# Two-layer hybrid decoder: triangular inverses started from 16x16 blocks made row by row, mixer products kept in DRAM until wanted, batch ends behind the next front, PSUM banks shared out anew

## The chip, the cores and the metric

One Trainium2 chip, one core of it. The metric is the device time of one execution in microseconds; before the change the median of 3 runs is 2915.05 us (2909.9 to 2915.27).

## The reference, cut to what matters

256 tokens of width 2048 in f32 pass two layers. Each layer has a token mixer and a SwiGLU part, each as `LayerNorm(ALPHA * x + (1 + gate(c)) * f(x * (1 + scale(c)) + shift(c)))`, where shift, scale and gate come from `silu(c) @ ada_w` (192 pieces of 1 MB). The mixer of layer 0 ("AB") is one input projection, then 8 mLSTM heads of width 128 beside 16 RWKV-7 heads of width 64, then one output projection. The mixer of layer 1 ("CD") has 8 retention heads beside 8 gated DeltaNet (GDN) heads. The two parts of it that the change is about:

```python
# RWKV-7, per head, over all 256 tokens
S_t = S_{t-1} (diag(w_t) - kk_t (a_t*kk_t)^T) + v_t k_t^T ;  y_t = S_t r_t
# gated DeltaNet, per head and chunk: a unit triangular solve
ut = eye + where(strict, (kb @ kc^T) * gamma, 0)
u, w = triangular_solve(ut, v * beta), triangular_solve(ut, kb * exp(gc))
```

Both need, for each head and each chunk of 128 tokens, the inverse of a unit triangular 128x128 matrix: 8 such matrices in each of 4 RWKV batches (4 heads by 2 chunks) and of 2 GDN groups.

## The kernel before, in words

**Products.** Every weight matrix goes through `split` (L325-341): a 1 MB piece `raw` is loaded by SP's queue, ACT copies it to `hi` (fp32r, L337) and DVE subtracts to `lo` (L338), and each product of 128 tokens by 512 columns is three matmuls, hi by hi, lo by hi, hi by lo (L357 to L359). `product` takes two banks of kind "g" in PSUM, one for each half of the tokens, and sums 4 pieces into them, 96 matmuls for 512 columns. Between the pieces `ada` does a share of the 192 adaLN pieces on DVE (L289). A splitting runs with a priority 2000 ahead of its place in the program, so DVE and ACT make `hi` and `lo` as far ahead as buffers allow. The order on each engine is set by the scheduler of the tile framework, from the program order and such offsets; the pools set when a buffer is free.

**Mixer AB** (L1263). `first_products` makes four products while the first weights arrive. `rwkv` then runs four batches. A batch is `rwkv_batch` (low-rank gates), two times `rwkv_front` (channel work on 128 channels), then `rwkv_heads`: score matrices (L776 to L779), the masks on POOL (`keep_upper` L642, `unit_diagonal` L646), `inverses` (L600), the chunk recurrence (L793 to L819), and, in the same function, the batch's end (head norm, gate, L821 to L845). Products 3, 4 and 5 of the RWKV columns stand in the program between the batches; then come the mLSTM gates (L906ff) and two groups of four mLSTM heads (`mlstm_group`, L973), each with its own four products (`product(0)` to `product(3)`) in front of and between its steps. `mix_out` is the output projection: its first half sums the RWKV channels (weights `o_ab`), its second half the mLSTM channels.

**An inverse** (L600-639). For 8 matrices `mt` (transposed, unit upper triangular), `d` holds the inverses of the diagonal blocks and `dt` their transposes, first of 2x2 blocks: 8 transposes of `mt` (L611), a mask on DVE (L612) and one on POOL (L613). Then six levels, each doubling the block: 8 matmuls of 64 columns (L622), a mask on DVE (L626), 8 more (L629), an addition on DVE (L632), 8 transposes (L636), two copies on ACT (L637). Each matmul of 64 columns is two records in the trace, a transpose is one.

**PSUM banks**: 4 of kind "g" (products), 3 of "m", 1 of "c".

## Time and profile before

| | before |
|---|---|
| median of 3 runs | 2915.05 us (2909.9 to 2915.27) |
| the profiled execution, its own time | 2917.53 us |
| its span, first to last instruction | 2914.8 us |
| mean granted TensorE clock | 0.976 of full speed |
| PE (TensorE) busy | 2760.8 us, 95% |
| DVE (VectorE) busy | 2011.9 us, 69% |
| ACT (ScalarE) busy | 1276.3 us, 44% |
| POOL (GpSimd) busy | 123.5 us, 4% |
| DMA | 674.62 MB, 231 GB/s over the span |

Busy shares are of the span. Matmuls overlap in the pipe, so a matmul's own duration (395 ns for 512 columns) is longer than the distance from one start to the next (227 ns), and it is the distances that add up to the time. The span begins with some 150 us in which weights arrive; mixer AB then lasts to about 800 us, a SwiGLU part to about 1530 us, mixer CD to about 2200 us, and a SwiGLU part to the end.

### The profile page before, as it was taken

How to read it: one execution, taken by the hardware profiler on the slowest of the kernel's cores; microseconds unless marked ns; L12 is line 12 of the kernel's file. 1: busy time of each engine (PE TensorE's matmuls, PEld its weight loads, DVE VectorE, ACT ScalarE, POOL GpSimd, SP SyncE). 2: the span in 40 equal slices, each digit the busy share in tenths (PEclk: the TensorE clock that was granted, in tenths of full speed). 3: DMA queues.
4: the chain of work that ended last, by engine and by line, in shares of the span. 5: the costliest groups of instructions: out<-in, count | busy, mean ns of one | idle time of the engine just before them, and what ended most of it. 6: DMA issues, size and time to landing. Idle time of an engine off the chain costs nothing.

```text
span 2914.8 us, 34843 instructions
## 1 busy us (share of the span) xinstructions
PE 2760.8 (95%) x13466; PEld 2291.6 (79%) x13466; DVE 2011.9 (69%) x2955; ACT 1276.3 (44%) x1685; POOL 123.5 (4%) x114
## 2 busy tenths in 40 slices
PE   3699999999999999999998999999989999999997
PEld 2578887877778888888887888877878888888886
DVE  7876666687777557767758878687786545556556
ACT  2264345446454444444445545343444444443442
POOL 0001111020000000000000121101000000000000
PEclk9799999999999999999999999999999999999998
DMA  9974234367578668867855756477656656667563
GB/s 366 356 277 170 91 134 159 131 242 267 199 249 305 249 219 296 297 236 275 305 197 205 295 209 241 159 277 295 216 202 231 249 195 224 242 220 241 192 216 130
DMA packets 106189, 674.62 MB, mean 231 GB/s; under 512 B 12068, under 2 KB 14248, under 8 KB 28328
## 3 DMA queue, kind: packets, MB, share of 16 engines
q1 hardware_dynamic: 106024, 672.41, 64.1%
q8 instruction: 105, 1.72, 0.2%
q14 instruction: 60, 0.49, 0.0%
HBM read 663.97 MB, written 8.39 MB: 231 GB/s over the span
## 4 chain that ended last, share of the span: by engine, by line
PE 62%; DVE 5%; DMA 3%; issue 1%; ACT 1%; POOL 1%; POOLq 0%; DVEq 0%; ACTq 0%
PE g L359 19%; PE g L358 19%; PE g L357 19%; DMA raw<-ada 2%; DVE lo L338 2%; DVE raw L289 1%; PE m L622 1%; PE m L629 1%; PE m L575 1%; ACT hi L337 1%; DMA raw<-gu 1%; DMA raw<-w_cd 0%; PE m L524 0%; PE c L317 0%; PE m L636 0%
## 5 line engine op out<-in xcount | busy, mean ns | idle before, releaser
L338 DVE TENSOR_TENSOR lo<-raw,hi 128x1024 fp32r<-128x1024 f32 (+2 forms) x848 | 1025.4, 1215 | 653.6 <-ACT hi L337 650.3
L337 ACT ACTIVATE hi<-raw 128x1024 fp32r<-128x1024 f32 (+2 forms) x848 | 885.7, 1049 | 1165.6 <-PE g L359 1004.1
L357 PE MATMUL g<-hi,h 128*128 128x512 f32 (+3 forms) x2368 | 932.7, 396 | 80.3 <-ACT hi L337 76.5
L358 PE MATMUL g<-lo,h 128*128 128x512 f32 (+3 forms) x2368 | 934.1, 395 | 3.8 <-DVE lo L338 3.8
L359 PE MATMUL g<-hi,h 128*128 128x512 f32 (+3 forms) x2368 | 930.9, 394 | 0.0
L357 PEld LDWEIGHTS g<-hi,h 128*128 128x128 f32 x2368 | 451.9, 191 | 172.0 <-ACT hi L337 78.8
L358 PEld LDWEIGHTS g<-lo,h 128*128 128x128 f32 x2368 | 452.6, 191 | 95.2 <-DVE lo L338 9.1
L359 PEld LDWEIGHTS g<-hi,h 128*128 128x128 f32 x2368 | 452.0, 191 | 88.6 <-issue 2.7
L289 DVE SCALAR_TENSOR_TENSOR raw<-raw,silu_c 128x2048 f32<-128x2048 f32 x176 | 404.4, 2298 | 23.1 <-DMA raw<-ada 22.8
L359 PE MATMUL g<-hi,a 128*128 128x512 f32 x960 | 374.5, 390 | 0.0
L357 PE MATMUL g<-hi,a 128*128 128x512 f32 x960 | 374.4, 390 | 0.0
L358 PE MATMUL g<-lo,a 128*128 128x512 f32 x960 | 374.1, 390 | 0.1
L358 PEld LDWEIGHTS g<-lo,a 128*128 128x128 f32 x960 | 180.3, 188 | 37.4 <-DVE lo L338 0.5
L359 PEld LDWEIGHTS g<-hi,a 128*128 128x128 f32 x960 | 180.3, 188 | 36.9
L357 PEld LDWEIGHTS g<-hi,a 128*128 128x128 f32 x960 | 180.2, 188 | 37.0
L1099 POOL TENSOR_SCALAR s<-cons_sb,log_alpha 128x128 f32<-128x128 f32 x16 | 22.9, 1446 | 1040.6 <-PE g L359 903.4
L637 ACT ACTIVATE y<-m 128x512 f32<-128x512 f32 x48 | 27.4, 595 | 78.3 <-PE m L636 78.1
L902 DVE SCALAR_TENSOR_TENSOR f<-c,cols_sb,f 128x255 f32<-128x255 f32 (+2 forms) x120 | 57.2, 477 | 6.2 <-ACT f L900 5.1
L626 DVE TENSOR_TENSOR P<-m,cons_sb 128x256 f32<-128x256 f32 x72 | 30.1, 423 | 43.6 <-PE m L622 43.2
L629 PEld LDWEIGHTS m<-P,y 128*128 128x128 f32 x384 | 50.0, 203 | 2.1 <-issue 0.3
L622 PEld LDWEIGHTS m<-y,a 128*128 128x128 f32 x384 | 49.7, 205 | 0.8
L622 PE MATMUL m<-y,a 128*128 128x64 f32 x384 | 49.7, 283 | 0.0
(376 smaller groups left out, 2051.2 us busy)
## 6 DMA issues: line engine op xcount, KB each, us to landing
raw<-ada SPq DMA_DIRECT2D x176, 1024.0 KB, 5.5
raw<-gu SPq DMA_DIRECT2D x176, 1024.0 KB, 4.8
raw<-dn SPq DMA_DIRECT2D x88, 1024.0 KB, 4.8
raw<-w_cd SPq DMA_DIRECT2D x60, 1024.0 KB, 5.0
raw<-w_ab SPq DMA_DIRECT2D x56, 1024.0 KB, 5.5
a<-ada SPq DMA_DIRECT2D x16, 1024.0 KB, 11.3
raw<-o_ab SPq DMA_DIRECT2D x16, 1024.0 KB, 5.0
raw<-o_cd SPq DMA_DIRECT2D x16, 1024.0 KB, 4.9
```

What stands on the lines that cost most here:

```text
L289: v.scalar_tensor_tensor(w[:], w[:], 1.0, self.sc[:], ALU.mult, ALU.mult, accum_out=m[:, i:i + 1])
L337: nc.scalar.activation(hi[:, :2 * n], ws, AF.Copy)
L338: nc.vector.tensor_tensor(lo[:, :2 * n], ws, hi[:, :2 * n], ALU.subtract)
L357: mm(o, ah, wh, start=first, stop=False)
L358: mm(o, ah, wl, start=False, stop=False)
L359: mm(o, al, wh, start=False, stop=stop and k == 3)
L575: nc.tensor.transpose(b[:, P * k:P * k + P], gs[:, t, P * k:P * k + P], self.ident)
L622: nc.tensor.matmul(x[:, 64 * j:64 * j + 64], mt[:, hs.start + j, :], dv[:, hs.start + j, :, 0, :], start=True, stop=True)
L626: v.tensor_tensor(p[-1][:], four(x[:, 0:256]), mask, ALU.mult)
L629: nc.tensor.matmul(x[:, 256 + 64 * j:320 + 64 * j], dt[:, hs.start + j, :], y[:, j, :], start=True, stop=True)
L637: nc.scalar.activation(dt[:, hs, :], four(x[:]), AF.Copy)
L902: v.scalar_tensor_tensor(o[:, d:T], z[:, 0:T - d], self.col(wname, c + 3 - d), o[:, d:T], ALU.mult, ALU.add)
```

## The change: what it does

1. `inverses`: levels 2, 4 and 8 go (`LEVELS` is now 16, 32, 64). The inverses of the 16x16 diagonal blocks are made on DVE. Four masks take the diagonal 16x16 blocks of `mt` into `e2`, two operations form `u` (strictly upper) and `e` (with the diagonal), and 14 steps follow, one for each row k of the block from 14 down to 1: STREAM_SHUFFLE copies row k of each block to the 16 rows of it, a multiplication by column k of `u`, an addition into `e`, each over 128 partitions by 8 matrices by n = 1 to 14 columns. Then `dt` is spread from `e` by two multiplications, transposed (8 transposes), and copied to `d` by ACT. The chain has a priority 4000 ahead. `unit_diagonal` and POOL's masking of `mt` go, as does POOL's L613; `keep_upper` stays for the other score matrices.
2. Mixer AB: the mLSTM gates come first. Products 3 and 4 of RWKV follow batch 0, product 5 follows batch 1, and the eight mLSTM products follow batches 1 (one), 2 (three) and 3 (four), behind the heads of each. Nine of these products are put by: `put_by` copies each bank on ACT into `sp` (one buffer), and ACT's queue writes it to DRAM; `fetch` loads it on SP's queue when wanted. A batch's end (`rwkv_out`) stands behind the next batch's front.
3. Banks: 3 "g", 3 "m", 2 "c". `q4` has 4 buffers instead of 5 and `t1` 3 instead of 4; `sz`, the mLSTM tokens and the low ranks move to other pools, and retention's output takes its values' buffer. The first products take kinds gg, gm, mm, cc.

With three banks a product's first tile often takes the bank that was read last: in the order of the change, in the SwiGLU part, tile g_1378's last matmul is PE row 3347 and the first of g_1401, which takes its bank, is row 3360; with four banks, before, g_1391's last is row 3343 and its successor's first row 3446. Such a turn of 12 to 13 rows is that of about every second tile of the 224.

The diff, cut to its core:

```diff
-LEVELS = (2, 4, 8, 16, 32, 64)
+BASE = 16
+LEVELS = (16, 32, 64)
...
-        self.ps_g = pool("psg", 4, space=PSUM)
+        self.ps_g = pool("psg", 3, space=PSUM)
...
-        self.ps_c = pool("psc", 1, space=PSUM)
+        self.ps_c = pool("psc", 2, space=PSUM)
...
@@ inverses
+        with self.tc.high_priority(offset=4000):
+            e2 = self.t1([P, 8, 2, BASE])
+            for q in range(4):
...
+                v.tensor_tensor(e2[r], mt[r, :, r].rearrange("p h (a c) -> p h a c", a=2),
...
+            u, e, f = (self.own([P, 8, BASE], "e1", 3) for _ in range(3))
+            v.tensor_tensor(u[:], e2[:, :, 0, :], e2[:, :, 1, :], ALU.add)
+            v.tensor_tensor(e[:], u[:], self.con("diag").unsqueeze(1).to_broadcast([P, 8, BASE]), ALU.add)
+            for k in range(BASE - 2, 0, -1):
+                n = BASE - 1 - k
+                x = f[:, :, k + 1:]
+                v.stream_shuffle(x, e[:, :, k + 1:], [k] * 16 + [16 + k] * 16)
+                v.tensor_tensor(x, x, u[:, :, k:k + 1].to_broadcast([P, 8, n]), ALU.mult)
+                v.tensor_tensor(e[:, :, k + 1:], e[:, :, k + 1:], x, ALU.add)
         for hs in halves:
+            v.tensor_tensor(dt[:, hs, :].rearrange("p h (n c) -> p h n c", c=BASE), e[:, hs, :].unsqueeze(2).to_broadcast([P, 4, 8, BASE]),
+                            self.con("blk").unsqueeze(1).unsqueeze(3).to_broadcast([P, 4, 8, BASE]), ALU.mult)
             b = self.bank()
             for j in range(4):
-                nc.tensor.transpose(b[:, P * j:P * j + P], mt[:, hs.start + j, :], self.ident)
-            v.tensor_tensor(d[:, hs, :], four(b[:]), m2, ALU.mult)
-            nc.gpsimd.tensor_tensor(dt[:, hs, :], mt[:, hs, :], m2t, ALU.mult)
+                nc.tensor.transpose(b[:, P * j:P * j + P], dt[:, hs.start + j, :], self.ident)
+            nc.scalar.activation(d[:, hs, :], four(b[:]), AF.Copy)
...
+    def put_by(self, banks):
+        dst = self.dram.tile([T, 512], F32, name=self.name("by"))
+        for t in range(NT):
+            s = self.own([P, 512], "sp", 1)
+            self.nc.scalar.activation(s[:], banks[t][:], AF.Copy)
+            self.nc.scalar.dma_start(dst[P * t:P * t + P, :], s[:])
+        return dst
...
@@ rwkv_heads
-            self.keep_upper(mk[:, :, js, :], [2, 4], True)
-            self.unit_diagonal(mk[:, 0, js, :], 4)
+            self.keep_upper(mk[:, 1, js, :], [4], True)
...
+        return lambda: self.rwkv_out(B, yb)
...
@@ rwkv
+        for i in range(5):
...
+            if out:
+                out()
+            if i < 4:
+                out = self.rwkv_heads(B)
+            if i == 0:
+                tokens += [self.by_tokens(product(3 + j)) for j in range(2)]
+            elif i == 1:
+                tokens.append(self.put_by(product(5)))
+            after(i)
...
@@ mixer_ab
+        def after(i):
+            for _ in range((0, 1, 3, 4, 0)[i]):
+                cols.append(self.put_by(product(6 + len(cols))))
+            if i >= 3:
+                self.mlstm_group(i - 3, cols[4 * i - 12:4 * i - 8])
```

How it moves instructions, at three places. First PE at the start of the first inverse, from the second set of 4 transposes on (`m` a bank, `y` holding `d` and `dt`, `a` the matrices `mt`, `P` the masked product). Before, with levels 2 and 4:

```order
L611 MATMUL m_1061<-cons_sb,a_993 128x128 x4
L622 MATMUL m_1068<-y_1053,a_993 128x64 x4
L691 MATMUL c_1435<-cons_sb,a_825 128x128
L357 MATMUL g_2832<-hi_2840,h_140 128x512
...
L622 MATMUL m_1073<-y_1053,a_993 128x64 x4
L629 MATMUL m_1068<-P_1078,y_1053 128x64 x4
L357 MATMUL g_2833<-hi_2840,h_140 128x512
L629 MATMUL m_1073<-P_1080,y_1053 128x64 x4
L636 MATMUL m_1092<-cons_sb,y_1053 128x128 x4
...
L636 MATMUL m_1098<-cons_sb,y_1053 128x128 x4
L622 MATMUL m_1104<-y_1053,a_993 128x64 x4
```

In the change the first level is that of 16 (L642 and L649 are its matmuls, L656 its transposes):

```order
L632 MATMUL m_1147<-cons_sb,y_1093 128x128 x4
L632 MATMUL m_1154<-cons_sb,y_1093 128x128 x4
L362 MATMUL g_2278<-hi_2281,h_140 128x512
L642 MATMUL m_1160<-y_1093,a_1039 128x64 x4
L642 MATMUL m_1165<-y_1093,a_1039 128x64 x4
L360 MATMUL g_2277<-hi_2285,h_140 128x512
L787 MATMUL c_1702<-f_1695,cons_sb 128x256
L649 MATMUL m_1160<-P_1170,y_1093 128x64 x4
L649 MATMUL m_1165<-P_1172,y_1093 128x64 x4
...
L656 MATMUL m_1184<-cons_sb,y_1093 128x128 x4
L656 MATMUL m_1190<-cons_sb,y_1093 128x128 x4
L642 MATMUL m_1196<-y_1093,a_1039 128x64 x4
```

The transposes (now L632) take `dt` (in `y_1093`) instead of the matrices, so they stand behind the chain on DVE; three of the six sets of L622, L629 and L636 are gone.

Second, DVE at the same place in the change: the chain ahead of those transposes (`e_205` is `u`, `e_206` is `e`, `e_207` the shuffled rows; `a_1039` holds the matrices, `s_1094` is `e2`).

```order
L616 TENSOR_TENSOR s_1094<-a_1039,cons_sb 32x256 x4
L341 TENSOR_TENSOR lo_1604<-raw_1597,hi_1603 128x1024
L619 TENSOR_TENSOR e_205_1099<-s_1094 128x128
L813 COPY a_1040<-m_1079 128x256
L620 TENSOR_TENSOR e_206_1100<-e_205_1099,cons_sb 128x128
L341 TENSOR_TENSOR lo_2121<-raw_2118,hi_2120 128x1024
L624 STREAM_SHUFFLE e_207_1101<-e_206_1100 128x8
L813 COPY a_1040<-m_1085 128x256
L625 TENSOR_TENSOR e_207_1101<-e_207_1101,e_205_1099 128x8
L311 SCALAR_TENSOR_TENSOR one_and_gate<-modulation,cols_sb 128x4
L626 TENSOR_TENSOR e_206_1100<-e_206_1100,e_207_1101 128x8
L292 SCALAR_TENSOR_TENSOR raw_2152,modulation<-raw_2152,silu_c 128x2048
```

Between its links stand other instructions that DVE has ready, `lo` (L341) of 128x1024 and `ada` (L292) of 128x2048. From the last score copy before it to `dt`, 10 to 14 of the first and 5 or 6 of the second stand in an RWKV batch, and on PE 160 to 180 product matmuls of 512 columns.

Third, PE at the mLSTM heads. Before, between a head's weights (L955 to L959) and its output (L1000 to L1002):

```order
L957 MATMUL m_4270<-minus_m,cons_sb 128x256
L958 MATMUL m_4270<-cons_sb,s_4267 128x128
L959 MATMUL m_4270<-minus_m,cons_sb 128x128
L969 MATMUL m_4280<-y_3574 128x256
L970 MATMUL m_4280<-y_3574 128x128
L357 MATMUL g_4436<-hi_4522,h_496 128x512
L358 MATMUL g_4436<-lo_4523,h_496 128x512
L359 MATMUL g_4436<-hi_4522,h_496 128x512
...
L357 MATMUL g_4435<-hi_4555,h_674 128x512
L1000 MATMUL m_4284<-q_4111,t_4276 128x129
L1001 MATMUL m_4284<-q_4111,t_4276 128x129
L1002 MATMUL m_4284<-q_4111,t_4276 128x129
```

In the change (L1000 to L1004 are the weights, L1014 and L1015 the scores, L1041 to L1043 the output):

```order
L1002 MATMUL m_4660<-minus_m,cons_sb 128x256
L1003 MATMUL m_4660<-cons_sb,s_4657 128x128
L1004 MATMUL m_4660<-minus_m,cons_sb 128x128
L1014 MATMUL m_4670<-y_4547 128x256
L1015 MATMUL m_4670<-y_4547 128x128
L1041 MATMUL m_4674<-q_4624,t_4666 128x129
L1042 MATMUL m_4674<-q_4624,t_4666 128x129
L1043 MATMUL m_4674<-q_4624,t_4666 128x129
L1000 MATMUL m_4688<-cons_sb,s_4685 128x256
L1001 MATMUL m_4688<-cons_sb,log_f 128x128
L1002 MATMUL m_4688<-minus_m,cons_sb 128x256
```

No product stands between the four heads of the first group (rows 1847 to 1881), and in the second group the four heads have 0, 17, 1 and 15 product matmuls between scores and output; before, the eight heads had 5 to 118. In the stretch from the end of the fourth inverse to the second half of the output projection the change has some 200 product matmuls, most of them `o_ab`'s first half; before, the eight mLSTM products, 768 matmuls, ran beside the mLSTM steps as well.

## Rows read from the trace of the kernel before

**Rows 1.** The page, parts 1 and 2: busy time of each engine with its share of the span and its instructions.

```profile
PE 2760.8 (95%) x13466; PEld 2291.6 (79%) x13466; DVE 2011.9 (69%) x2955; ACT 1276.3 (44%) x1685; POOL 123.5 (4%) x114
```

**Rows 2.** Windows of the core: the stretch in us, busy us of PE, weight load, DVE, ACT and POOL (in brackets the instructions), granted TensorE clock, DMA share, GB/s. The first stretch is the load at the start, the others are the RWKV batches.

```profile
50.00:100.00 50.00, 29.30 (x125) 24.09 (x123) 42.74 (x47) 9.56 (x12) 0.00 (x0) 0.79 0.94 367
150.00:350.00 200.00, 191.79 (x1080) 159.32 (x1078) 137.24 (x253) 100.29 (x176) 22.12 (x18) 0.96 0.54 192
300.00:350.00 50.00, 46.48 (x257) 38.45 (x255) 29.71 (x64) 21.94 (x50) 10.30 (x9) 0.86 0.37 127
350.00:550.00 200.00, 194.00 (x1257) 166.28 (x1258) 125.94 (x292) 92.42 (x177) 21.59 (x19) 0.97 0.35 123
500.00:550.00 50.00, 47.29 (x328) 43.50 (x327) 27.89 (x55) 20.32 (x33) 6.97 (x8) 0.90 0.26 91
```

**Rows 3.** Timeline of PE in the SwiGLU part of layer 0: start us, duration us, engine, line, operation.

```profile
1000.01 0.39 PE L359 MATMUL g<-hi,a 128*128 128x512 f32 x1
1000.24 0.39 PE L357 MATMUL g<-hi,a 128*128 128x512 f32 x1
```

**Rows 4.** Timeline of PE in the first inverse, the same columns; x is how many records in a row.

```profile
250.68 1.90 PE L622 MATMUL m<-y,a 128*128 128x64 f32 x16
252.41 1.08 PE L724 MATMUL c<-cons_sb,b 128*128 128x256 f32 x4
...
256.05 1.04 PE L636 MATMUL m<-cons_sb,y 128*128 128x128 f32 x8
256.93 1.00 PE L622 MATMUL m<-y,a 128*128 128x64 f32 x8
```

**Rows 5.** The groups of PE by line, whole span: busy us, mean ns of one, idle us before and its releaser. The three levels' lines, for the RWKV batches (`y`) and the GDN groups (`a`).

```profile
L622 PE MATMUL m<-y,a 128*128 128x64 f32 x384 | 49.7, 283 | 0.0
L629 PE MATMUL m<-P,y 128*128 128x64 f32 x384 | 49.6, 284 | 0.0
L636 PE MATMUL m<-cons_sb,y 128*128 128x128 f32 x192 | 28.0, 280 | 0.0
...
L622 PE MATMUL m<-a,a 128*128 128x64 f32 x192 | 23.3, 272 | 0.0
L629 PE MATMUL m<-P,a 128*128 128x64 f32 x192 | 22.9, 271 | 0.0
...
L636 PE MATMUL m<-cons_sb,a 128*128 128x128 f32 x96 | 13.3, 273 | 0.0
```

**Rows 6.** The waits of the whole span: engine, tile and line, what it waited for, us in total, times, longest us.

```profile
ACT hi L337 <- PE g L359: 1004.1, 657, 8.4
...
PE m L524 <- DVE v L492: 18.5, 3, 6.2
...
PE m L611 <- POOL a L646: 16.9, 8, 3.9
```

**Rows 7.** The groups of DVE by line and shape, the same columns as in the groups of PE.

```profile
L338 DVE TENSOR_TENSOR lo<-raw,hi 128x1024 fp32r<-128x1024 f32 x824 | 1008.8, 1229 | 649.7 <-ACT hi L337 646.5 <-PE c L895 0.5
L289 DVE SCALAR_TENSOR_TENSOR raw<-raw,silu_c 128x2048 f32<-128x2048 f32 x176 | 404.4, 2298 | 23.1 <-DMA raw<-ada 22.8
...
L626 DVE TENSOR_TENSOR P<-m,cons_sb 128x256 f32<-128x256 f32 x72 | 30.1, 423 | 43.6 <-PE m L622 43.2
...
L632 DVE TENSOR_TENSOR y<-m,y 128x256 f32<-128x256 f32 x48 | 20.3, 424 | 25.2 <-PE m L629 24.8
...
L612 DVE TENSOR_TENSOR y<-m,cons_sb 128x512 f32<-128x512 f32 x8 | 5.5, 690 | 8.9 <-PE m L611 8.9
...
L412 DVE TENSOR_TENSOR v<-v 128x8 f32<-128x8 f32 x30 | 4.9, 164 | 0.5
...
L1191 DVE SCALAR_TENSOR_TENSOR s<-s,s 128x128 f32<-128x128 f32 x3 | 0.9, 291 | 0.1
```

**Rows 8.** The groups of ACT by line and shape, the same columns.

```profile
L637 ACT ACTIVATE y<-m 128x512 f32<-128x512 f32 x48 | 27.4, 595 | 78.3 <-PE m L636 78.1
```

**Rows 9.** Timeline of PE and DVE at the first two mLSTM heads: L970 is the end of a head's scores, L997 its weights times scores, L1000 its output; in square brackets idle us before and the releaser.

```profile
593.02 0.38 PE L970 MATMUL m<-y 128*128 128x128 f32 x2
...
598.17 0.80 PE L1000 MATMUL m<-q,t 128*128 128x129 f32 x2 [3.15 <-DVE t L997]
...
603.20 0.38 PE L970 MATMUL m<-y 128*128 128x128 f32 x2
...
604.61 0.56 DVE L997 SCALAR_TENSOR_TENSOR t<-m,t 128x384 f32<-128x384 f32 x1 [1.44 <-POOL t L642]
```

**Rows 10.** Timeline of PE, ACT and DVE at the end of products in the SwiGLU part: a product's last matmul into a bank, the copy that frees the bank, and the same on DVE (L572).

```profile
965.04 0.39 PE L359 MATMUL g<-hi,h 128*128 128x512 f32 x1
...
965.46 0.60 ACT L568 ACTIVATE q<-g 128x512 f32<-128x512 f32 x1 [0.30 <-PE g L359]
...
986.96 1.23 DVE L338 TENSOR_TENSOR lo<-raw,hi 128x1024 fp32r<-128x1024 f32 x1 [1.49 <-ACT hi L337]
988.10 1.28 DVE L572 TENSOR_TENSOR q<-g,q 128x512 f32<-128x512 f32 x2
```

**Rows 11.** The view of the DMA: issues by line and tile, KB each, median us from issue to landing (writes of 256 KB to DRAM).

```profile
x<-y SPq DMA_DIRECT2D x24, 256.0 KB, 2.8
```

More of the change, by code (lines that the diff above doesn't have):

```diff
@@ L46 @@
 _n = 0
-for _name, _w in [("ident", 128), ("cum", 256), ("tr", 128), ("ones", 128), ("sl", 128), ("m2", 128), ("m2t", 128),
+for _name, _w in [("ident", 128), ("cum", 256), ("tr", 128), ("ones", 128), ("sl", 128), ("tri", 32), ("diag", 16), ("blk", 8),
                   ("lev", 64 * len(LEVELS)), ("bones", 128), ("hsel", 2), ("freq", 64)]:
@@ L69, in constants @@
     put("sl", u > t)
-    put("m2", (u // 2 == t // 2) & (t <= u))
-    put("m2t", (u // 2 == t // 2) & (u <= t))
+    c32, c16 = np.arange(32)[None], np.arange(BASE)[None]
+    put("tri", (u % 32 // BASE == c32 // BASE) & (u % BASE < c32 % BASE))
+    put("diag", u % BASE == c16)
+    put("blk", u // BASE == np.arange(P // BASE)[None])
     lev = []
@@ L682, in by_tokens, with fetch @@
         return zt
+    def put_by(self, banks):
[5 more added lines that the diff above has]
+        return dst
+    def fetch(self, out, src):
+        for t in range(NT):
+            rows = src[P * t:P * t + P, :]
+            self.nc.sync.dma_start(out[:, t], rows if len(out.shape) == 3 else rows.rearrange("p (h d) -> p h d", h=4))
     def rwkv_tiles(self, zt, block):
         nc = self.nc
+        if block == 5:
+            src, zt = zt, self.own([P, NT, 512], "zt", 2)
+            self.fetch(zt, src)
         for i in range(0, 4, 2):
@@ L833, in rwkv_heads @@
                                  bias=va[:, j:j + 1], scale=rs[:, j:j + 1])
-        b = self.bank()
+        b = self.bank("c")
         for c in range(2):
@@ L853, in first_products @@
         srcs = [[low[i] for i in range(KG)]] + [[w[4 * b + i] for i in range(KG)] for b in range(3)]
-        banks = [[self.bank(k) for k in kinds] for kinds in ("gg", "gg", "mm", "mc")]
+        banks = [[self.bank(k) for k in kinds] for kinds in ("gg", "gm", "mm", "cc")]
         h = []
@@ L862, in first_products, with rwkv, conv @@
         return h, [banks[0], self.by_tokens(banks[1])] + [self.by_tokens(banks[2 + i], two[:, i]) for i in range(2)]
-    def rwkv(self, h, rate, early):
+    def rwkv(self, product, early, after):
         self.rkv = {}
         self.rwkv_low(early[0])
-        w = self.ins["w_ab"]
+        self.mlstm_gates()
+        nc = self.nc
         tokens = early[1:]
-        B = None
-        c = made = 0
-        for i in range(4):
-            while len(tokens) < (3, 3, 5, 6)[i]:
-                blk = len(tokens)
-                tokens.append(self.by_tokens(self.product([w[4 * blk + k] for k in range(KG)], 512, h, rate)))
-            B = self.rwkv_batch(i)
-            for c in (2 * i, 2 * i + 1):
-                while 4 * made < 3 * c + 3:
-                    self.rwkv_tiles(tokens[made], made)
-                    made += 1
-                self.rwkv_front(B, c)
-            if i % 2 == 0:
-                self.yT[2 + i // 2] = self.a8([P, 2, 4, T], F32R)
-            self.rwkv_heads(B)
-    def conv(self, banks, outs, wname, tile0):
+        made = 0
+        out = None
+        for i in range(5):
+            if i < 4:
+                B = self.rwkv_batch(i)
+                for c in (2 * i, 2 * i + 1):
+                    while 4 * made < 3 * c + 3:
+                        self.rwkv_tiles(tokens[made], made)
+                        made += 1
+                    self.rwkv_front(B, c)
+                if i % 2 == 0:
+                    y = self.yT[2 + i // 2] = self.a8([P, 2, 4, T], F32R)
+                    nc.gpsimd.memset(y[:, 0, 0, 0:1].bitcast(F32), 0.0)
+            if out:
+                out()
+            if i < 4:
+                out = self.rwkv_heads(B)
[4 more added lines that the diff above has]
+            after(i)
+    def conv(self, zt, outs, wname, tile0):
         nc, v = self.nc, self.nc.vector
-        zt = self.by_tokens(banks)
         for i in range(0, 4, 2):
@@ L1264, in mixer_ab, with product @@
         self.yT = {}
-        self.rwkv(h, rate, early)
-        self.mlstm_gates()
-        for g in range(2):
-            self.mlstm_group(g, self.ins["w_ab"], h, rate)
+        w = self.ins["w_ab"]
+        cols = []
+        def product(b):
+            return self.product([w[4 * b + k] for k in range(KG)], 512, h, rate)
+        def after(i):
[3 more added lines that the diff above has]
+                self.mlstm_group(i - 3, cols[4 * i - 12:4 * i - 8])
+        self.rwkv(product, early, after)
     def mixer_cd(self, h, rate):
```

53 lines of the change are left out of this document (25 added, 28 removed).

## The prediction

> **What bounds the kernel now.** I read the page first: PE is busy 95% of the span, DVE 69%, ACT 44%, POOL 4% [rows 1]. So the time goes where PE's time goes, unless an edit makes PE wait. Then the windows: while the weights first arrive PE is busy 29 of 50 us, and in the 400 us of the RWKV batches 191.79 and 194.00 of 200, so only 14 us of idle are to be had there [rows 2]. The timeline of a dense stretch gives the price of a product matmul of 512 columns: 0.23 us from one start to the next, not its duration of 0.39 [rows 3]. The same reading inside an inverse gives the price of a level [rows 4]. The waits show that PE's one systematic wait around the inverses is for POOL, 16.9 us in all, and that ACT, which makes `hi`, spends 1004 us waiting for PE [rows 6]: the splitting runs ahead of PE, and small delays on ACT or DVE reach PE only where that lead is used up.
>
> The profiled execution took 2917.5 us by its own time (span 2914.8), 2.5 above the median of 2915.05. The sum is made against 2917.5, and the 2.5 is taken off at the end. About 0.2% (6 us) is what a measurement of this kernel can tell from no change.
>
> **The change, part by part.**
>
> *Levels 2, 4 and 8 on PE.* One level is 16 records of L622, 16 of L629 and 8 of L636. Sixteen of L622 take 252.41 - 250.68 = 1.73 us; L629 has the same mean (284 against 283 ns), so 1.73 as well; eight of L636 take 256.93 - 256.05 = 0.88 [rows 4, 5]. Together 4.34 us. Three levels in six inverses are 18: **-78 us**. PE is full beside them with product matmuls that only move up, so the gain is real where PE stays full. By the records' durations the six levels are 186.8 us [rows 5], half of it 93; that counts the overlap of the pipe twice and is the far end. The near end is -60: in the inverse some of the removed time was a filler for a wait that stays.
>
> *POOL.* The transposes of the matrices no longer wait for POOL's masks: 16.9 us of wait in that form goes [rows 6]. What is late next is the DVE chain (below). I take **-12**; ends -17 and 0.
>
> *TensorE's clock.* The windows with an inverse's start show a granted clock of 0.86 and 0.90 [rows 2]. At 1.2 GHz instead of 2.4 for 28% and 20% of 50 us, PE loses at most 7 and 5 us. Fewer waits there give some of it back: **-5**; ends -12 and +5.
>
> *The DVE chain.* Each inverse gains 14 steps of three operations on 128 partitions by 8 to 112 elements. The trace has no shuffle; the nearest rows for all three are 164 ns at 8 columns and 291 ns at 128 [rows 7]. The mean step is at 60 columns, between them: 42 by 0.22 is about 9 us; ends 42 by 0.164 = 6.9 and 42 by 0.291 = 12.2. The masks and `dt` add 4 by 0.42, two small ones and 2 by 0.69, some 4 us; three levels of 2 by (0.423 + 0.424) and two operations of 0.69 go, 6.5 us [rows 7]. DVE has then about 6 us more per inverse, 38 in all on an engine that idles 31%. On the path it is the length of the chain that counts. In an RWKV batch the order puts 10 to 14 `lo` (1.23 us) and 5 or 6 `ada` (2.30 us) between its links [rows 7]: 9 + 4 + 12 by 1.23 + 5.5 by 2.30 is about 41 us, against 160 to 180 product matmuls of 0.227 us on PE, 36 to 41 us [rows 3]. So it is nearly covered. I take 1 us for each RWKV batch, none for the GDN groups: **+4**; ends 0 and +20. If the products ran out, all 41 us would be seen.
>
> The Trainium skill (VectorE: DVE Perf Modes, Rules for kernel authors) speaks against such a chain: every DVE operation drains the pipe, so in chained operations the count is to be kept down. The row of 164 ns for 8 columns agrees, since 16 times the columns cost only 1.8 times as much. By that rule alone 252 small operations for 18 levels would be a bad trade; by the sum it is one, only where DVE's time is not covered.
>
> *The mLSTM steps without their products.* Before, products stood between a head's scores and its output. In the change six of the eight heads have none or one there. Where seven product matmuls did not suffice, PE sat 3.15 us until 598.17, and from the scores' end at 593.40 it was 4.8 us; in the next head the output's operand was ready at 605.17, 1.6 us after the scores' end at 603.58 [rows 9]. So a bare head costs 1.6 to 4.8 us; six by 3.2 is 19. Each group also ends with a norm on DVE in front of its transposes; the nearest wait of PE for such a norm is at most 6.2 us [rows 6], and before, products filled it in part. I take 1 us for both: **+20**; ends 0 and 6 by 4.8 + 2 by 6.2 = +41.
>
> *Products put by.* Nine products by two copies of 0.6 us on ACT [rows 8]; some replace copies that were there. The second copy has one buffer `sp` and so waits for the first's write, 2.8 us [rows 11]. Behind it on ACT wait the next `hi`, and the bank stays taken meanwhile. Nine by 2.8 is 25 us of ACT; with 1004 us of ACT waiting for PE it mostly hides: **+5**; ends 0 and +25. The fetches, nine times 512 KB on SP's queue, stand behind weight loads and in front of others: no cost by themselves where DMA has room, 0.35 to 0.54 busy in the batches [rows 2].
>
> *Three banks for products.* Every second tile, 112 of 224, takes a bank whose last matmul is only 12 product matmuls back, 12 by 0.227 = 2.7 us [rows 3]. ACT freed one at 966.06, 1.0 us after its last matmul's start at 965.04; on DVE two in a row take 1.28 us, and may stand behind a `lo` of 1.23 [rows 10], 2.5 us. It just fits. **+4** for those behind an `ada`; the far end is a rival.
>
> *Batch ends behind the next front.* The 14 us of idle in the batches [rows 2] are nearly all POOL's, so **-2**.
>
> Sum: -78 - 12 - 5 + 4 + 20 + 5 + 4 - 2 = -64. 2917.5 - 64 - 2.5 is **2851 us**.
>
> **The rivals.**
>
> *The mLSTM stretch starves, and the clock with it* (2880). For it: DVE gets as much work there as PE, since the splitting and `ada` of the next weights run in it. The far end of the heads is +41 instead of +20. And PE with gaps has been granted 0.79 at the start, where it is busy 29 of 50 us [rows 2]; PE work of some 86 us (200 product matmuls are 45 of it) at 0.79 takes 23 us longer. Half of the latter with the former gives +31. Against: the heads are independent and may overlap. Chance 0.20. The Trainium skill (TensorE: Matmul & The Clock Gate, HAM oscillation) describes matmul loops that idle between bursts and start each burst cold; the window at the start agrees, and by it this rival's clock term would come in full.
>
> *DVE becomes the bound of the RWKV batches* (2888). At 0.34 a step (above the far row) and an `ada` in front of each link the chain is 46 us against 36 on PE: +9 or 10 in each of four batches. Chance 0.05.
>
> *More than the sum* (2815). The levels give 93, the waits of POOL and the clock all of theirs (17 and 12), the heads overlap. 2915 minus 122 plus some 20 for the rest is about 2815. For it: levels are chains between PE, DVE and ACT, whose cost beyond PE's own time also goes. Chance 0.16.
>
> *Slower: three banks* (2930). If the banks come free later than 2.7 us, behind a `lo` and an `ada` (1.23 + 2.30 + 0.68 = 4.2 us [rows 7, 10]), every such turn stalls PE. At 0.75 us for each of 112 turns that is +84, and eats the gain with 15 to spare. The point from which it decides is 64/112 = 0.57 us a turn. Against: ACT frees most banks in 1 us, and DVE idles. Chance 0.06.
>
> *Nothing to see* (2915). The removed levels only lay beside waits of the chain, and PE waits as long for DVE as it computed before. Chance 0.04; against it stands that PE is full in those stretches.
>
> **How the numbers follow.** The forecast itself has 0.49 (2830 to 2870). The range 2810 to 2888 takes in it, the starved stretch, DVE as the bound and most of the larger gain, and leaves out the two last rivals and some of the tails. All cases but those two are faster by over 0.2%: 0.90 faster, 0.04 the same, 0.06 slower.
>
> **What would show it.** Right: L642, L649 and L656 of the changed kernel with half the records of L622, L629 and L636; no wait of PE for POOL in the inverses; PE busy about 80 us less, the SwiGLU parts unchanged within some us. The heads show in the waits as PE L1041 waiting for DVE. Wrong: a wait of a product's first matmul for ACT or DVE evictions of tens of us (banks); transposes L632 waiting more than 5 us for DVE each (chain); a granted clock well under 1 in the mLSTM stretch; a mixer CD that loses as much as AB gains.

## The result, and the profile after

The changed kernel takes 2879.53 us (median of 4 runs, 2876.98 to 2886.5), before 2915.16 in the same comparison: a ratio of 0.988 with an interval of 0.986 to 0.991, or 36 us less. The forecast was 2851 with a range of 2810 to 2888, so the direction and the range held, but little more than half of the 64 us came: the time is that of the first rival, 2880. The profiled execution of the change took 2886.5 us, 7 above its median; its span is 2884.8. One of the four runs of the kernel with two products put by, below, took 4556.8 us at a granted clock of 0.555, and its ratio leaves that run out.

First the page's busy times of the change, to be read against [rows 1]:

```profile
PE 2699.7 (94%) x12746; PEld 2216.1 (77%) x12746; DVE 2035.7 (71%) x3255; ACT 1260.7 (44%) x1663; POOL 73.8 (3%) x88
```

PE is busy 61 us less, where 78 were priced for the levels, and the span is only 30 us shorter: the other 31 have come back as time in which PE waits. The lines of the three levels, RWKV part, groups of PE by line, against [rows 5]:

```profile
L642 PE MATMUL m<-y,a 128*128 128x64 f32 x192 | 23.5, 271 | 0.5 <-ACT y L633 0.5
L649 PE MATMUL m<-P,y 128*128 128x64 f32 x192 | 23.0, 271 | 0.0
...
L656 PE MATMUL m<-cons_sb,y 128*128 128x128 f32 x96 | 13.0, 273 | 0.0
```

Half the records and a little less than half the time, as forecast. The wait for POOL of [rows 6] has gone. The new links of the chain, groups of DVE by line and shape, against the 164 and 291 ns of [rows 7]:

```profile
L624 DVE STREAM_SHUFFLE e<-e 128x112 f32<-128x112 f32 x6 | 1.7, 291 | 0.0
...
L625 DVE TENSOR_TENSOR e<-e,e 128x112 f32<-128x112 f32 x6 | 1.6, 269 | 0.1
...
L626 DVE TENSOR_TENSOR e<-e,e 128x56 f32<-128x56 f32 x6 | 1.3, 215 | 0.1
...
L624 DVE STREAM_SHUFFLE e<-e 128x8 f32<-128x8 f32 x6 | 1.1, 186 | 0.0
...
L625 DVE TENSOR_TENSOR e<-e,e 128x8 f32<-128x8 f32 x6 | 1.0, 166 | 0.0
```

The shuffle (L624) costs 20 ns more than the multiplication (L625) of the same shape, and the mean link is about 0.23 us, where 0.22 was taken. From the first mask (L616) to the end of `dt` (L628) the chain lasts 39 to 42 us in the four batches, where the forecast has 41. So the length of the chain was right.

Where the time went is seen by stages. AB is counted from the span's start to the first gate copy on ACT of the first SwiGLU part, CD from the last such copy of that part to the first of the second; all from the profiled executions. The prediction's terms are split as 12 and 6 of the 18 levels and 9 and 3 of POOL's 12 us:

| us | AB | first SwiGLU | CD |
|---|---|---|---|
| before | 831.9 | 627.2 | 725.1 |
| the change | 815.3 | 628.2 | 710.7 |
| sum of the prediction's terms | -39 | 0 | -29, and +4 of banks anywhere |
| measured | -17 | +1 | -14 |

Each stage is read from one execution. That of the change lies 7 us above its median, and in which stage those 7 us lie is not known, so differences of a few us between stages are not resolved. Windows of AB (columns as in [rows 2]) from 150 us to its end, then of CD, each time first before and then the change:

```profile
150.00:831.90 681.90, 655.41 (x3595) 542.40 (x3594) 484.89 (x992) 337.55 (x566) 64.59 (x62) 0.97 0.52 186
150.00:815.30 665.30, 615.65 (x3114) 492.53 (x3113) 503.60 (x1192) 331.01 (x554) 32.56 (x47) 0.94 0.57 205
```

```profile
1459.10:2184.20 725.10, 692.55 (x3549) 579.30 (x3548) 560.88 (x974) 333.07 (x485) 58.75 (x48) 0.98 0.64 230
1443.50:2154.20 710.70, 669.32 (x3307) 551.89 (x3306) 567.71 (x1076) 324.57 (x476) 40.93 (x36) 0.98 0.65 234
```

In AB PE is idle for 50 us instead of 26, 23 more, where the sum's terms for waits (POOL, chain, heads and norms, products put by, batch ends) make 18. Its busy time falls by 40 us, where levels and clock were to take 52 + 5 = 57. So the larger part of what AB misses lies in the busy time, and there the granted clock went from 0.97 to 0.94: some 40 us at 1.2 GHz have become some 80. An estimate from these rows: 40 us more at half the clock lose at most 20 us, which is enough for the 17 that are missing. In CD the clock is the same; PE is busy 23 us less, where 26 were forecast, and idle 41 us instead of 33. Part of the idle is the chain on DVE, of which the sum books nothing in CD: the products wait longer for `lo`, first before, then in the change.

```profile
PE g L358 <- DVE lo L338: 1.4, 3, 0.5
```

```profile
PE g L361 <- DVE lo L341: 7.1, 9, 1.7
```

With half of the chain left out (below) this wait is 1.5 us in the same order.

Shorter windows of the change, first the RWKV batches, then the mLSTM steps:

```profile
150.00:350.00 200.00, 194.17 (x981) 153.03 (x980) 169.93 (x386) 110.26 (x186) 8.93 (x11) 1.00 0.70 255
350.00:550.00 200.00, 195.00 (x1074) 158.96 (x1073) 161.30 (x400) 92.74 (x165) 10.79 (x11) 0.99 0.63 228
600.00:650.00 50.00, 39.18 (x154) 29.96 (x153) 21.19 (x70) 20.46 (x36) 5.82 (x12) 0.71 0.18 64
650.00:700.00 50.00, 33.53 (x127) 23.87 (x128) 25.66 (x88) 28.31 (x49) 5.69 (x11) 0.68 0.07 22
```

In the batches PE is busy 194 and 195 of 200, a little more than before, at a clock of 1.00 and 0.99, and DVE has risen from 137 and 126 to 170 and 161. PE loses nothing there. But from 600 to 700 us PE is busy 73 of 100, its granted clock is 0.71 and 0.68, and the DMA share is 0.18 and 0.07. Finer windows of the same stretch:

```profile
620.00:630.00 10.00, 7.80 (x23) 5.46 (x21) 4.80 (x14) 3.98 (x8) 0.41 (x1) 0.50 0.01 2
630.00:640.00 10.00, 8.96 (x27) 6.93 (x28) 1.52 (x6) 1.26 (x4) 0.41 (x1) 0.50 0.00 0
640.00:650.00 10.00, 5.10 (x20) 3.63 (x18) 4.41 (x32) 1.35 (x4) 0.41 (x1) 0.67 0.00 0
650.00:660.00 10.00, 2.20 (x8) 1.43 (x8) 8.56 (x45) 2.57 (x5) 1.27 (x3) 0.50 0.31 104
```

Between 620 and 640 PE's records fill 78 and 90% and the clock is yet 1.2 GHz: there are only the small matmuls of the heads, with short gaps. These shares are those of records that are themselves longer at that clock, as the timeline below shows. The waits of PE from 550 to 720 us:

```profile
PE m L958 <- DVE q L1062: 8.1, 2, 7.4
PE c L875 <- ACT t L870: 5.7, 1, 5.7
PE c L940 <- DVE f L947: 5.3, 2, 3.3
...
PE m L1041 <- DVE t L1038: 4.3, 4, 1.8
```

L1041 is a head's output waiting for its weights: 4.3 us in all, not the 3.2 for each of six heads of the forecast. The long waits are at the ends: 8.1 for the first group's norm (L958), 5.7 for batch 3's end (L875), 5.3 in the convolutions (L940). The larger part of a head's cost is the clock, as the timeline shows: it fell beside a wait of PE of 2.0 us, in the first row (granted clock 1.00 from 610 to 617 us, 0.51 from 617 to 641); the next four rows are at 1.2 GHz, the last at 2.4.

```profile
618.23 1.08 PE L940 MATMUL c<-cons_sb,y 128*128 128x128 f32 x4 [2.02 <-DVE f L947]
...
623.93 1.06 PE L1000 MATMUL m<-cons_sb,s 128*128 128x256 f32 x2
...
628.96 0.64 PE L1015 MATMUL m<-y 128*128 128x128 f32 x2
630.32 0.80 PE L1041 MATMUL m<-q,t 128*128 128x129 f32 x2 [0.73 <-DVE t L1038]
...
631.77 1.06 PE L1000 MATMUL m<-cons_sb,s 128*128 128x256 f32 x2
...
701.26 0.60 PE L1000 MATMUL m<-cons_sb,s 128*128 128x256 f32 x2
```

A set of L1000 takes 1.06 us at the low clock and 0.60 at the high one.

### The profile page after: what moved, and what is told of

Same layout as the page of the kernel before. It is cut to its first block, busy times and chain, and to the rows that moved or that the text cites. A ratio compares the mean times of both kernels' runs of the same rounds, so it can differ in the third digit from the quotient of the medians.

```text
span 2884.8 us, 33590 instructions
## 1 busy us (share of the span) xinstructions
PE 2699.7 (94%) x12746; PEld 2216.1 (77%) x12746; DVE 2035.7 (71%) x3255; ACT 1260.7 (44%) x1663; POOL 73.8 (3%) x88
## 4 chain that ended last, share of the span: by engine, by line
PE 58%; DVE 8%; DMA 4%; issue 1%; ACT 1%; POOL 0%; POOLq 0%; DVEq 0%; ACTq 0%
PE g L361 18%; PE g L362 18%; PE g L360 18%; DVE lo L341 3%; DMA raw<-ada 2%; DVE raw L292 2%; DMA raw<-gu 1%; ACT hi L340 1%; PE m L578 1%; DMA raw<-w_cd 1%; DMA t<-x 1%; PE m L527 0%; PE c L320 0%; PE m L642 0%; PE m L649 0%
## 5 line engine op out<-in xcount | busy, mean ns | idle before, releaser
L341 DVE TENSOR_TENSOR lo<-raw,hi 128x1024 fp32r<-128x1024 f32 (+2 forms) x848 | 1024.2, 1213 | 650.0 <-ACT hi L340 647.5
L360 PE MATMUL g<-hi,h 128*128 128x512 f32 (+3 forms) x2352 | 923.1, 394 | 85.7 <-ACT hi L340 81.0
L362 PE MATMUL g<-hi,h 128*128 128x512 f32 (+3 forms) x2352 | 921.4, 392 | 0.0
L360 PEld LDWEIGHTS g<-hi,h 128*128 128x128 f32 x2352 | 447.3, 191 | 181.2 <-ACT hi L340 85.3
L362 PEld LDWEIGHTS g<-hi,h 128*128 128x128 f32 x2352 | 447.6, 190 | 88.4 <-issue 3.2
L292 DVE SCALAR_TENSOR_TENSOR raw<-raw,silu_c 128x2048 f32<-128x2048 f32 x176 | 403.1, 2290 | 31.1 <-DMA raw<-ada 30.5
L947 DVE SCALAR_TENSOR_TENSOR f<-c,cols_sb,f 128x253 f32<-128x253 f32 (+2 forms) x120 | 53.5, 475 | 13.4 <-ACT f L945 13.1
L530 ACT ACTIVATE t<-m,affine 128x128 f32<-128x128 f32 x96 | 35.0, 474 | 29.9 <-PE m L527 26.4
L403 ACT ACTIVATE t<-t,affine 128x256 f32<-128x256 f32 x16 | 8.7, 588 | 76.4 <-DVE affine L301 76.4
L292 DVE SCALAR_TENSOR_TENSOR a<-a,silu_c 128x2048 f32<-128x2048 f32 x16 | 36.6, 2287 | 0.4
L527 PE MATMUL m<-cons_sb,y 128*128 128x128 f32 x96 | 16.9, 319 | 18.4 <-DVE v L495 18.4
L527 PEld LDWEIGHTS m<-cons_sb,y 128*128 128x128 f32 x96 | 13.3, 167 | 23.1 <-issue 20.2
```

Of the source, the lines that this page charges most:

```text
L292: v.scalar_tensor_tensor(w[:], w[:], 1.0, self.sc[:], ALU.mult, ALU.mult, accum_out=m[:, i:i + 1])
L341: nc.vector.tensor_tensor(lo[:, :2 * n], ws, hi[:, :2 * n], ALU.subtract)
L360: mm(o, ah, wh, start=first, stop=False)
L362: mm(o, al, wh, start=False, stop=stop and k == 3)
L403: nc.scalar.activation(h32[:, j, :], x[:, j, :], AF.Identity, bias=self.ab[:, 16 + k:17 + k], scale=self.ab[:, k:k + 1])
L527: nc.tensor.transpose(b[:, P * j:P * j + P], y[t][:, P * k:P * k + P], self.ident)
```

## The experiments

Theory A at the start: the levels are worth what PE's time for them says, and the mLSTM steps, bare of products, lost the difference. Rivals: the chain on DVE gives back half of the levels; the third bank costs the missing part of CD; a fetch on SP's queue starves the stretch. Times are medians with the ratio to before and its interval.

**One half of the change each.** The first kernel is the one before with the new `inverses` alone, the second the change with the old ones:

```diff
 # e1: before.py             # e2: after.py
-LEVELS = (2, 4, 8, 16, 32, 64)
+LEVELS = (16, 32, 64)
...                          # e2: the same hunk reversed
```

> The kernel before with the new inverses alone (16x16 blocks row by row, three levels); order of mixer AB and banks as before. Theory A, the levels are worth what PE's time for them says (78 us, and the waits for POOL of some 10 us), and the change lost the difference to the mLSTM steps without products: 2830 us (2815 to 2845). Rival B, the DVE chain gives back half of the levels in every inverse, and the reordering is about neutral: 2870 to 2885, as the change. Rival C, half of the loss is of the reordering and half of the pools: 2840 to 2865. In mixer CD, which this kernel has with the old pools, A and C expect a gain of 26 to 30 us from the levels, B the 14 us that the change gained.

> The change with the old inverses (six levels, POOL's masks): the new order of mixer AB, products put by, and the new banks and pools. Theory A: slower than before, 2945 us (2930 to 2965), with TensorE at the lower clock in the mLSTM stretch as in the change. Rival B (reordering neutral, the chain eats the gain): 2905 to 2920. If the two edits add, this kernel and the one with the levels alone are together as far from before as the change is.

Measured: levels alone 2867.5 us (0.984, 0.983 to 0.986); order and banks alone 2969.0 (1.019, 1.017 to 1.022). Every range was missed, 2867.5 between those of C and B, 2969.0 just above that of A. The levels are worth 48 us in the old order and 2969.0 - 2879.5 = 89 us in the new one. The new order and banks cost 53 us with the old inverses and 12 with the new. So the edits do not add, and the change as it stands is slower than the levels alone (the intervals, 0.9825 to 0.9855 and 0.9859 to 0.9907, just do not meet). By stages, levels alone give 24.8 us in AB and 23.7 in CD; order and banks alone cost 46.5 in AB and 9.0 in CD. The window of AB of order and banks alone, to be read against that of before:

```profile
150.00:878.40 728.40, 675.54 (x3598) 548.75 (x3597) 492.38 (x992) 340.09 (x570) 58.66 (x63) 0.93 0.53 188
```

PE has the work of before there, 3598 records against 3595. It is idle 26 us longer, near the 23 of the forecast's terms for heads and norms, products put by and batch ends, and busy 20 us longer at a clock of 0.93 instead of 0.97, which the forecast did not have. Not all of the 20 need be the clock: a record that no other overlaps counts with its whole length. Windows of the kernel with the levels alone:

```profile
300.00:350.00 50.00, 35.60 (x152) 26.16 (x152) 30.48 (x122) 18.88 (x47) 3.94 (x5) 0.69 0.16 51
400.00:450.00 50.00, 42.49 (x177) 30.67 (x175) 42.70 (x119) 25.09 (x50) 6.15 (x5) 0.90 0.60 210
500.00:550.00 50.00, 45.59 (x176) 33.12 (x177) 38.66 (x109) 21.78 (x44) 4.05 (x6) 0.84 0.42 158
```

Three of its batches have a bare stretch of their own, with waits of PE that the change does not have in the same stretch (150 to 640 us):

```profile
PE m L853 <- ACT t L848: 8.6, 2, 8.0
PE c L708 <- DVE e L624: 7.7, 2, 5.9
PE c L911 <- DVE v L418: 7.6, 1, 7.6
```

L853 is a batch's end (the change has that wait once, 5.7 us, behind its last batch), L708 RWKV's transposes, released by a link of the chain, and L911 the transposes of an mLSTM convolution, released by DVE at L418.

**Half of the chain left out**, in either order:

```diff
-            for k in range(BASE - 2, 0, -1):
+            for k in range(BASE - 2, 0, -2):
```

> The kernel with the new inverses alone, in which 7 of the 14 row steps are left out (the inverses are then not those of the reference): the chain on DVE is 21 operations shorter, 4.6 us by 0.22 each, and what the queue puts between them. Theory F, in the old order the chain lies on the path of the RWKV batches, and that is where the missing 30 us of the levels went: 15 to 25 us faster than with the whole chain, 2848 us (2842 to 2855), with the batches' distances shorter by 4 us or more each. Rival I, the batches are held up elsewhere (batch ends and fronts without products), the chain is covered: 2862 to 2870.

> The change, in which 7 of the 14 row steps are left out (the inverses are then not those of the reference). Theory F: the put-by products cover the chain, so it is worth nothing: 2880 us (2874 to 2886). Rival J, the chain is on the path here too: 20 us faster or more, 2860.

Measured: 2841.4 us (0.975, 0.973 to 0.976), 26 less than the whole chain in the old order, of it 19.7 in AB and 6.7 in CD by the profiled executions; in the change 2878.8 (0.988, 0.986 to 0.989), no difference. So in the old order the chain lies on the path, theory F; in the change it is covered, and a shorter chain is worth nothing. That is shown for the chain's length; how much of the rest is the batch ends' place was not separated.

**Products back in the mLSTM steps.** Of the second group all four; of both groups all but two; all eight:

```diff
-            for _ in range((0, 1, 3, 4, 0)[i]):
+            for _ in range((0, 1, 3, 0, 0)[i]):   # e3; (0, 1, 1, 0, 0) in e10; (0, 0, 0, 0, 0) in e11
                 cols.append(self.put_by(product(6 + len(cols))))
...                                               # mlstm_group makes those that are not put by
```

> The change, but the four products of the second mLSTM group are not put by: they stand in that group again, as before the change; the first group's are put by. Theory A, PE has nothing to fill the heads and norms with: the stretch from 612 to 700 us gets 87 us of products back, its clock stays near 1, the idle of 27 us goes by half or more, while batch 3 loses a filler: 2850 us (2840 to 2865). Rival D, what starves the stretch is a fetch that waits for a buffer on SP's queue and holds up the weight loads behind it (39.8 us in the trace of the change): these loads are no longer behind such a fetch, so the same gain, but then the stretch shows product matmuls of the output projection early. Rival B: within 8 us of the change, 2872 to 2888.

> The change, but of the eight mLSTM products only the first two are put by, and six stand in their groups again; the order of the batches and the three product banks are the change's. In the order on PE the eight heads have 30, 29, 12, 13, 4, 25, 3 and 25 product matmuls between scores and output, where the change has 0, 0, 0, 0, 0, 17, 1 and 15. Theory A, it is the missing products in the mLSTM steps: AB gains 15 to 30 us on the change, no stretch of 50 us falls below 45 of PE busy or a clock of 0.9 for that reason: 2856 us (2845 to 2866). Theory F sets the limit: as few products are left for batch 3, its chain shows, at most 10 us. Rival L, what the heads gain the batches lose in full: 2870 to 2885.

> As the last, with none of the eight mLSTM products put by, all in their groups; the batch ends behind the next front, the early gates and the banks stay the change's. Against the kernel with the new inverses alone it shows what the batch ends and the RWKV products' places are worth. Theory F, with no products put by the batches have too few to cover the chain: 5 to 15 us slower than with two put by, 2865 us (2855 to 2875). Rival M, the scheduler brings the first group's products forward by itself: as with two put by or faster, 2845 to 2855.

Measured: 2870.2 us (0.985, 0.983 to 0.987), 2866.0 (0.983, 0.981 to 0.985) and 2863.1 (0.982, 0.980 to 0.984). They beat the change by 9 to 16 us, the last two with intervals that do not meet the change's; AB is 802.8, 800.0 and 798.8 instead of 815.3. Theory A has the sign right, and the gains that it gave lie above or at the edge of what came. The windows tell why, first with the second group's products in place, then with two products put by, then with none:

```profile
600.00:650.00 50.00, 38.88 (x136) 28.48 (x137) 25.83 (x104) 18.21 (x36) 3.90 (x8) 0.64 0.12 43
650.00:700.00 50.00, 49.98 (x256) 40.69 (x255) 35.89 (x77) 39.58 (x60) 9.93 (x9) 1.00 0.48 173
```

```profile
400.00:450.00 50.00, 37.95 (x159) 28.17 (x159) 34.02 (x137) 17.21 (x43) 4.31 (x5) 0.69 0.10 39
450.00:500.00 50.00, 45.99 (x235) 37.48 (x234) 20.67 (x82) 19.19 (x50) 2.43 (x4) 0.70 0.00 1
600.00:650.00 50.00, 49.99 (x226) 39.39 (x225) 47.70 (x117) 24.49 (x36) 6.81 (x6) 1.00 0.79 295
```

```profile
300.00:350.00 50.00, 41.83 (x189) 31.55 (x188) 37.85 (x140) 18.74 (x44) 4.55 (x6) 0.78 0.31 111
450.00:500.00 50.00, 45.66 (x276) 36.30 (x276) 29.60 (x104) 20.96 (x53) 3.91 (x6) 0.86 0.13 43
600.00:650.00 50.00, 49.93 (x228) 39.62 (x227) 47.57 (x90) 27.85 (x46) 10.92 (x7) 1.00 0.83 304
```

The mLSTM steps are dense where the products are back: 650 to 700 in the first, 600 to 650 in the two others. But each kernel has its bare stretch elsewhere, at the first group, at 400 to 500, or at 300 to 350 and 450 to 500, with the clock at 0.64 to 0.86 and a DMA share of 0.00 to 0.31. Mixer AB has only so many products, and they are spent wherever PE finds them ready; putting them by lets PE spend them early and leaves a hole at the end. That the rows show; that no order could cover both the batches and the mLSTM steps is not shown. None put by came at the time that theory F gave, but not slower than two put by: its limit did not show, and rival M is right on the order of the two, not on the size.

**Is it the waits or the clock?** Matmuls that nobody reads, in PE's gaps:

```diff
+    def keep_busy(self, n):
+        x = self.h0
+        b = self.bank()
+        for _ in range(n):
+            self.nc.tensor.matmul(b[:], x[:, 0, 0, 0:P], x[:, 0, 0:2, :].rearrange("p k t -> p (k t)"), start=True, stop=True)
...
             b = self.scores(qt[:, j, :], kt[:, j, :])
+            self.keep_busy(6)
...
+        self.keep_busy(32)
...
+        self.h0 = h[0]
```

> The change with 112 added matmuls of 128x512 in the mLSTM steps whose result nobody reads: 6 behind each head's scores and 32 ahead of each group's norm, 25 us of PE by 0.227 us each. They lie where PE waits. Theory A2, the granted clock of 0.5 to 0.7 doubles the small matmuls of the heads, and the waits themselves are only some 27 us: with PE busy the clock stays near 1 from 610 to 700 us, and the stretch is shorter by 8 to 18 us in spite of the added work: 2867 us (2860 to 2876). Rival H, the heads are bound by the chain over ACT, POOL and DVE, and the clock costs nothing: the clock rises, the time stays or grows by up to 15 us (2878 to 2895).

Measured: 2890.3 us (0.991, 0.989 to 0.993), 11 slower than the change. Windows and the timeline of PE at two heads (L1000, the added matmuls L1022, the next L1000):

```profile
600.00:650.00 50.00, 45.22 (x217) 34.83 (x215) 26.51 (x99) 20.35 (x36) 6.33 (x12) 0.97 0.19 69
650.00:700.00 50.00, 37.33 (x138) 26.02 (x139) 22.72 (x70) 26.59 (x49) 6.13 (x12) 0.69 0.09 27
```

```profile
630.49 0.60 PE L1000 MATMUL m<-cons_sb,s 128*128 128x256 f32 x2
...
633.59 1.65 PE L1022 MATMUL m<-h 128*128 128x512 f32 x6
...
635.74 0.60 PE L1000 MATMUL m<-cons_sb,s 128*128 128x256 f32 x2
```

The clock of 600 to 650 rose from 0.71 to 0.97, and one head follows the next after 635.74 - 630.49 = 5.3 us, added matmuls included, where the change takes 631.77 - 623.93 = 7.8. So at the first group's heads the clock was the price, as theory A2 said. The total went the other way: the clock of 650 to 700 stayed at 0.69, and of 25 us added AB shows 9.6. The trace has 39 of the 112 added matmuls behind 700 us, where PE is busy without a gap in the change as well (14.00 us of 700 to 714). An estimate, 39 by 0.227, is 8.9 us, most of what AB lost; the other 73 then cost nothing in sum. Rival H's range holds the time, but its ground, that the clock costs nothing, is refuted at these heads. What the clock costs in the whole kernel was not measured apart.

**The fetch on SP's queue.** In the change, waits of SP's queue from 550 to 720 us:

```profile
SPq L327 <- DVE lo L341: 64.7, 5, 42.8
SPq L713 <- DVE q L1062: 39.8, 1, 39.8
```

```diff
-        self.fetch(so, cols[2])
+        self.fetch(so, cols[2], nc.gpsimd)
...
-        self.fetch(va[:, :, :, 0:P], cols[3])
+        self.fetch(va[:, :, :, 0:P], cols[3], nc.gpsimd)
```

> The change with the fetches of the mLSTM output gates and values on POOL's queue instead of SP's; in the change one of them waits 39.8 us for a buffer on SP's queue, with the last two weight pieces of the output projection's first half behind it. Theory D, this wait starves the stretch: the two pieces arrive by 630 us, 48 product matmuls (11 us) come into the stretch, and it is 8 to 15 us shorter: 2868 us (2862 to 2873). Rival K, the products of that projection are held by buffers and order, and the stretch is bare because only 200 matmuls are left for it: within 5 us of the change, 2875 to 2885.

Measured: 2883.3 us (0.990, 0.988 to 0.992), the change's time. The wait is only replaced (570 to 720 us):

```profile
SPq L327 <- DVE lo L341: 98.4, 3, 88.0
```

The loads now wait for `lo` instead; why `lo` is late there stays open. The fetch is not the cause.

**The banks.**

```diff
-        self.ps_g = pool("psg", 3, space=PSUM)
+        self.ps_g = pool("psg", 4, space=PSUM)
...
-        self.ps_c = pool("psc", 2, space=PSUM)
+        self.ps_c = pool("psc", 1, space=PSUM)
...
```

> The change with the banks as before: four for products, three, and one for the rest; batch ends take their banks from the three. Theory E, three banks cost nothing, since the SwiGLU parts of the change take as long as before to 0.5 us: 2880 us (2872 to 2888). Rival C, the 13 us that mixer CD lost against the sum are of the third bank: 2867 (2860 to 2872), all of the gain in CD.

> Two put by as above, with the banks as before the change (4, 3, 1). Theory E2, the banks cost 11 us in CD and give 7 in AB: 3 to 8 us faster than with three product banks, 2851 us (2840 to 2862). Rival: no difference within 3 us.

Measured: 2881.2 us (0.989, 0.987 to 0.991) and 2879.0 (0.989, 0.987 to 0.991). The first total is what theory E said, for another reason: CD takes 699.6 us instead of 710.7, and AB 822.8 instead of 815.3. With two put by it is 699.2 instead of 707.5 in CD and 813.5 instead of 800.0 in AB. The medians are 13 apart there, with intervals that do not meet, and the stages only 5, since the profiled execution with four banks lies 7 below its median. Theory E2 is wrong in the sum. One row of CD for the change and one for four banks:

```profile
1455.00:2145.00 690.00, 648.62 (x3216) 534.78 (x3215) 555.85 (x1065) 315.39 (x465) 40.93 (x36) 0.98 0.64 234
```

```profile
1460.00:2140.00 680.00, 644.40 (x3218) 533.18 (x3217) 556.98 (x1064) 315.28 (x464) 45.04 (x36) 0.98 0.66 238
```

PE is idle 41 us in the first and 36 in the second.

**The first group behind batch 2**, and the old banks from CD on:

```diff
-            if i >= 3:
-                self.mlstm_group(i - 3, cols[4 * i - 12:4 * i - 8])
+            if i == 2 or i == 4:
+                self.mlstm_group(i // 2 - 1, cols[2 * i - 4:2 * i])
...
+        k.banks(4, 3, 1)
         k.ada_limit = 176
```

> The change with two edits that show in different stages: the first mLSTM group stands behind batch 2 instead of batch 3, so that batch 3 and the second group's four products lie beside its heads; and before mixer CD the PSUM banks are shared out as before the change (4, 3, 1). Theory A: only the second group is left bare, 10 to 20 us less until the first SwiGLU part; theory of the third bank: 9 to 11 us less in CD. Together 2855 us (2845 to 2865). Rival G, batch 3 loses to the first group what that gains: AB as in the change, 2870 (2866 to 2876).

Measured: 2913.4 us (1.000, 0.999 to 1.002). AB is 843.2: batch 3's first scores came some 90 us later than in the change, so rival G, only worse. CD was 708.5, hardly shorter than with three banks. Where the pools change, between 1520 and 1600 us, the transposes of the LayerNorm wait for its other steps (L533 for L528 and L536) as in no other kernel, and PE waits 14.5 us in all, where the change waits 10.9 from 1490 to 1590. That makes some 4 us of the 8 to 11 that four banks give in CD in the runs above; the rest stays open.

## Why the prediction was right or wrong

The direction held, and the time lies in the range near its far end; the forecast itself was 28 us too low.

- **Levels, POOL and chain** (-78 - 12 + 4 = -86): 89 measured in the change's own order, the clock's share included. The PE time of a level, the end of POOL's wait and the length of the chain were right there. In the old order the same edit gave 48, and half of the chain is worth 26. "Nearly covered" was true of the products that the new order puts beside the chain, and the prediction read it from the change's order. In CD, where it booked nothing for the chain, the wait for `lo` rose by 5.7 us.
- **TensorE's clock** (-5; ends -12 and +5): this is the step that failed. The sum took fewer waits for a better clock, looked only at the windows where an inverse starts, and left the mLSTM steps to the first rival. There the clock was at its lower level for most of the first group's heads: AB had some 80 us at 1.2 GHz instead of some 40, by the estimate above up to 20 us instead of a gain of 5, and with the old inverses the new order made PE busy 20 us longer over the same work. The prediction's own sign of being wrong, a granted clock well under 1 in the mLSTM stretch, came: 0.71 and 0.68.
- **The mLSTM steps without products, and products put by** (+20 and +5): with none of the eight put by the kernel is 16 us faster, so the two terms together were not too small. How they are made up was wrong: the heads' waits for their weights are 4.3 us in all where 19 were taken, the first group's norm 8.1 and the second's none where 1 was taken for both, and the convolutions, which the sum does not have, 5.3. That the waits of AB came to 23 in all, near the 18 of the sum, is in part luck. ACT's copies wait 17.7 us for their writes, below the 25 of the far end; PE shows no wait that is put down to them.
- **Three banks** (+4): none of it where it was sought, in the SwiGLU parts, which take 627.2 and 628.2 us. In CD three banks cost some 8 to 11 us between kernels that have the one or the other throughout, and in AB they gain 7 to 13 over four, which the prediction did not see.
- **Batch ends** (-2): not measured apart. One wait of 5.7 us for a batch's end stands behind the last batch.
- **The rivals**: the first named heads, norms and clock, and its 2880 us was the time. By its terms AB would be 8 us shorter than before and CD 25 to 29, where 17 and 14 were measured, so that the time is met exactly is in part luck. DVE as the bound of the batches is refuted by the half chain in the change; its 46 us hold the 5.5 `ada` of the sum and not one in front of each link, as its text has it. The slower one with three banks is refuted by the SwiGLU parts (its +84 less the gain of 64 would leave 20 to spare, not 15), "nothing to see" by the interval. The larger gain came in no kernel; 2841.4 with half of the chain is the lowest.
- The Trainium skill (VectorE: DVE Perf Modes, Rules for kernel authors) says that in chained operations the count is what to keep down. The runs bear it out in the old order, where half the links are worth 26 us, and not in the change, where they are worth nothing.
- The Trainium skill (TensorE: Matmul & The Clock Gate, HAM oscillation) ties the slow clock to idle gaps between bursts of matmuls. The trace of the change agrees in that the clock fell beside a wait of 2.0 us. It then stayed at its lower level through 20 us in which PE's records fill 78 and 90% and no wait is above 1.8 us, and with 512-column matmuls in these gaps it was 0.97 from 600 to 650 us.

## What to carry to other kernels

Count the large matmuls that a stage has left as cover before moving them: here a product moved from one chain of small steps to another covered the new one and bared the old one, and the bare one paid twice, in waits and in the granted clock. Cost an edit inside the order it will run in; here the same inverses are worth 48 us in one order and 89 in another. And change one thing at a time: the inverses alone, or the change with the mLSTM products left in place, are faster than the whole change.

## What was not expected of the hardware

STREAM_SHUFFLE of 128 partitions takes 186 ns for 8 columns and 291 for 112, where a multiplication takes 166 and 269. PE's granted clock was 0.50 over 20 us in which its records fill 78 and 90%, with no wait above 1.8 us in the heads of that stretch.
